# Depthwise convolution of a projection read straight from PSUM, block boundaries convolved together

## Chip, cores and metric

One NeuronCore of a Trainium2 chip runs the whole program. The metric is the device time of one execution in microseconds (us). The engines are named as in the profile: PE is TensorE (matrix products), PEld its weight loads, DVE is VectorE, ACT is ScalarE, POOL is GpSimd, SP is the queue that issues nearly all DMAs. Every engine works through its own instructions in a fixed order, and waits at one whose inputs or buffers aren't ready.

## What is computed

The reference is one layer of an encoder on 2048 tokens of width 1024: a normalised input goes through one projection, whose columns feed neighbourhood attention, an mLSTM and a gated delta rule; then come an output projection, cross-attention and a feed-forward layer. The change touches the delta rule's input alone: 1152 projected columns (q, k, v) go through a centred depthwise convolution over five tokens and a SiLU.

```python
def centred_depthwise_conv(x, w):
    c = x.shape[-1]
    return lax.conv_general_dilated(
        x, w[:, None, :].astype(x.dtype), window_strides=(1,),
        padding=[(CONV_K // 2, CONV_K // 2)],
        dimension_numbers=('NWC', 'WIO', 'NWC'), feature_group_count=c)
...
    qkv = jax.nn.silu(centred_depthwise_conv(jnp.concatenate([q, k, v], axis=-1), conv_w))
    qc, kc, vc = jnp.split(qkv, 3, axis=-1)
```

Token t of the output needs tokens t-2 to t+2 of the projection, so an output next to the boundary of two blocks of tokens needs projections of both blocks.

## The kernel before

The kernel is written in a framework that takes the program in the order of its source, gives each engine a fixed list of instructions by a list scheduler (earlier source goes first where several are ready), and sets the semaphores. Channels lie on the 128 partitions, tokens along the free dimension, everything in fp32; products are split in a high and a low part and take three passes.

`pass_a` (L153) is the stage around the change. It goes over four blocks of 512 tokens (b = 0 to 3). For each block it runs nine channel tiles (ct = 0 to 8) of `gdn_in` (L282); after tile 2 it normalises the next block's input (`norm_in`, L239), after tile 6 it makes the gates (`gates`, L335). Then come the Gram matrices of the block's pairs of chunks (`gram`, L412), which read the convolved q, k, v back from DRAM (`gd_c`), with projections of the mLSTM and of the attention (`ml_in`, `rest`) between them. The inverses of a group (`inv`, L475: 30 steps of two small DVE instructions for each direction, L495 and L496) stand in the source ahead of the next block, so they run on DVE beside the next block's convolutions.

One tile of `gdn_in` before the change:

- `wtile` (L982 on): the weights are loaded by SP, cast to `whi` on ACT (L987); the rest `wlo` is made by a POOL subtraction (L989) of 128 x 1024 elements from SBUF.
- `gemm` (L1018): 24 matmuls of 128 x 512 (L108) into a PSUM tile of the pool `psg`, which has two buffers, one bank each. The gates, the mLSTM and the attention projections use the same two.
- L295: ACT copies the bank to the SBUF tile `pad`, columns 4 to 515. The bank is free once that copy is done.
- L299 and L303: DVE copies the four tokens before the block in from `edge`, and this tile's last four tokens out to `edge` (27 each; memsets, L297 and L301, stand in at both ends of the sequence).
- L306 and L308: DVE multiplies by the first tap and adds the other four, five instructions with `pad` and `acc` in SBUF.
- L310: ACT makes the tanh; L311: DVE makes the SiLU (doubled) of it; L312: SP stores the tile to `gd_c`, two tokens behind the projection.

`pad`, `acc` and `th` have two buffers each (`cp`, L160).

## Time and profile before

| what | value |
|---|---|
| time, median of 3 runs | 3787.74 us (3775.37 to 3800.31) |
| span of the profiled execution | 3789.0 us |
| PE busy over the span | 3468.7 us (92%) |
| DVE busy over the span | 1819.1 us (48%) |
| ACT busy over the span | 1153.2 us (30%) |
| POOL busy over the span | 1601.0 us (42%) |

Busy shares are means over a program whose stages have different limits, so the stage of the change, the first 620 us, is to be read by itself. A busy PE is not a PE at its peak: matmuls overlap, and the clock that it is granted changes with what it did before. "Idle before" names what an engine waited for; it costs something only where that engine, or one that waits for it, sets the end.

### The profile page before, as it was taken

How to read it: one execution, taken by the hardware profiler on the slowest of the kernel's cores; microseconds unless marked ns; L12 is line 12 of the kernel's file. 1: busy time of each engine (PE TensorE's matmuls, PEld its weight loads, DVE VectorE, ACT ScalarE, POOL GpSimd, SP SyncE). 2: the span in 40 equal slices, each digit the busy share in tenths (PEclk: the TensorE clock that was granted, in tenths of full speed). 3: DMA queues.
4: the chain of work that ended last, by engine and by line, in shares of the span. 5: the costliest groups of instructions: out<-in, count | busy, mean ns of one | idle time of the engine just before them, and what ended most of it. 6: DMA issues, size and time to landing. Idle time of an engine off the chain costs nothing.

```text
span 3789.0 us, 54073 instructions
## 1 busy us (share of the span) xinstructions
PE 3468.7 (92%) x21392; PEld 2774.0 (73%) x21392; DVE 1819.1 (48%) x3257; ACT 1153.2 (30%) x2015; POOL 1601.0 (42%) x947
## 2 busy tenths in 40 slices
PE   5878688888788889999999999999999999999998
PEld 4656566666666655588888887888888778888887
DVE  7697977625666644553443436222222352222224
ACT  3233232232323333544343344222222332222223
POOL 4455444554454531253535445333333453333333
PEclk9988888988899996999999999999999999999999
DMA  4546475678999565742233233111111141111112
GB/s 140 179 132 183 140 193 142 174 181 200 202 215 217 173 216 172 210 174 98 95 134 134 87 123 133 53 45 48 45 50 48 60 138 48 49 53 48 53 47 89
DMA packets 396663, 466.07 MB, mean 123 GB/s; under 512 B 151978, under 2 KB 296826, under 8 KB 393338
## 3 DMA queue, kind: packets, MB, share of 16 engines
q1 hardware_dynamic: 392794, 450.55, 41.2%
q0 software_dynamic: 3616, 12.06, 0.9%
q8 instruction: 169, 2.77, 0.3%
q14 instruction: 84, 0.69, 0.1%
HBM read 360.01 MB, written 102.50 MB: 122 GB/s over the span
## 4 chain that ended last, share of the span: by engine, by line
PE 52%; DVE 1%; ACT 1%; issue 1%; DMA 0%; POOL 0%; POOLq 0%; DVEq 0%; SPq 0%; ACTq 0%
PE psg L108 31%; PE psa L108 21%; PE psa L1180 0%; DVE nh L1005 0%; DVE ss L1016 0%; PE psm L88 0%; PE psm L99 0%; ACT whi L987 0%; DMA out_y<-nh 0%; DMA xb<-x_d 0%; POOL wlo L989 0%; DVE xb L1251 0%; ACT acta L1137 0%; ACT acta L1006 0%; ACT sqt L1015 0%
## 5 line engine op out<-in xcount | busy, mean ns | idle before, releaser
L989 POOL TENSOR_TENSOR wlo<-wraw,whi 128x1024 fp32r<-128x1024 f32 (+2 forms) x401 | 842.0, 2101 | 1294.1 <-ACT whi L987 1271.7
L108 PE MATMUL psg<-acta,whi 128*128 128x512 f32 x3008 | 975.3, 404 | 36.9 <-ACT pad L295 23.2
L108 PE MATMUL psg<-actb,whi 128*128 128x512 f32 (+2 forms) x2752 | 857.4, 393 | 36.8 <-DVE rt L613 10.2
L987 ACT CAST whi<-wraw 128x1024 fp32r<-128x1024 f32 (+2 forms) x417 | 373.5, 896 | 1192.3 <-PE psa L108 551.7
L108 PEld LDWEIGHTS psg<-acta,whi 128*128 128x128 f32 x3008 | 576.7, 194 | 169.2 <-ACT pad L295 25.2
L108 PE MATMUL psa<-ht,whi 128*128 128x512 f32 x2048 | 638.6, 395 | 0.6 <-ACT whi L987 0.5
L108 PEld LDWEIGHTS psg<-actb,whi 128*128 128x128 f32 (+1 forms) x2752 | 518.9, 193 | 148.2 <-ACT pad L295 11.2
L108 PE MATMUL psg<-acta,wlo 128*128 128x512 f32 x1504 | 602.5, 402 | 3.6 <-POOL wlo L989 3.6
L108 PE MATMUL psg<-actb,wlo 128*128 128x512 f32 (+2 forms) x1376 | 539.9, 393 | 27.9 <-POOL wlo L989 27.9
L108 PEld LDWEIGHTS psa<-ht,whi 128*128 128x128 f32 x2048 | 384.0, 188 | 95.1 <-ACT whi L987 1.5
L1229 DVE TENSOR_TENSOR fr<-fr 128x512 f32<-128x512 f32 x128 | 167.9, 1312 | 495.4 <-ACT fr L1228 495.4
L1242 DVE TENSOR_TENSOR xb<-psa,xb 128x512 f32<-128x512 f32 x256 | 175.6, 691 | 476.4 <-PE psa L108 476.3
L108 PE MATMUL psa<-ht,wlo 128*128 128x512 f32 x1024 | 401.0, 396 | 0.7 <-POOL wlo L989 0.7
L108 PEld LDWEIGHTS psg<-acta,wlo 128*128 128x128 f32 x1504 | 290.8, 193 | 67.6 <-POOL wlo L989 5.0
L108 PEld LDWEIGHTS psg<-actb,wlo 128*128 128x128 f32 (+1 forms) x1376 | 265.2, 193 | 86.5 <-POOL wlo L989 33.4
L1232 POOL TENSOR_TENSOR ht<-fr,ht 128x512 fp32r<-128x512 f32 x128 | 169.1, 1321 | 249.1 <-ACT ht L1231 247.8
L108 PEld LDWEIGHTS psa<-ht,wlo 128*128 128x128 f32 x1024 | 192.3, 188 | 47.5 <-POOL wlo L989 1.8
L1016 DVE TENSOR_TENSOR ss<-ss,sqt 128x512 f32<-128x512 f32 (+1 forms) x91 | 123.4, 1356 | 47.0 <-ACT sqt L1015 44.3
L308 DVE SCALAR_TENSOR_TENSOR acc<-pad,vecs,acc 128x512 f32<-128x512 f32 (+2 forms) x144 | 143.6, 1000 | 1.5 <-DVE sm L436 0.6
L1231 ACT CAST ht<-fr 128x512 fp32r<-128x512 f32 x128 | 79.4, 621 | 180.1 <-DVE fr L1229 180.0
L1228 ACT ACTIVATE fr<-psg 128x512 f32<-128x512 f32 x128 | 75.9, 593 | 132.3 <-PE psg L108 132.3
L495 DVE TENSOR_TENSOR tv<-x 72x30 f32<-72x30 f32 (+36 forms) x210 | 94.4, 470 | 2.0 <-DVE x L496 0.6
(376 smaller groups left out, 3982.3 us busy)
## 6 DMA issues: line engine op xcount, KB each, us to landing
wraw<-in_w_ff SPq DMA_DIRECT2D x72, 512.0 KB
wraw<-in_w_ff SPq DMA_DIRECT2D x144, 256.0 KB
wraw<-in_w_gd SPq DMA_DIRECT2D x36, 512.0 KB
sc_d<-sc SPq DMA_DIRECT2D x32, 576.0 KB
xt<-in_xT SPq DMA_DIRECT2D x16, 1024.0 KB
wraw<-in_w_out SPq DMA_DIRECT2D x32, 512.0 KB
wraw<-in_w_xq SPq DMA_DIRECT2D x32, 512.0 KB
wraw<-in_w_xo SPq DMA_DIRECT2D x32, 512.0 KB
```

The costliest lines, as they stand in the source:

```text
L108: nc.tensor.matmul(out=out, lhsT=a(k), rhs=b(k), start=(i == 0), stop=(i == n - 1))
L308: V.scalar_tensor_tensor(out=acc[:, :n], in0=pad[:, p0 + j:p0 + j + n], scalar=cw(j), in1=acc[:, :n], op0=ALU.mult, op1=ALU.add)
L495: V.tensor_tensor(out=tv, in0=m[:, j + 1:32, j:j + 1].broadcast_to([2 * N, n, j]), in1=m[:, j:j + 1, 0:j].broadcast_to([2 * N, n, j]), op= ...
L987: nc.scalar.copy(out=hi, in_=raw)
L989: (lo_eng or nc.gpsimd).tensor_tensor(out=lo, in0=raw, in1=hi.bitcast(F32), op=ALU.subtract)
L1016: nc.vector.tensor_tensor(out=ss, in0=ss, in1=sq, op=ALU.add)
L1228: S.activation(out=r, in_=ps, func=AF.Relu)
L1229: V.tensor_tensor(out=r, in0=r, in1=r, op=ALU.mult)
L1231: S.copy(out=ht[:, 0], in_=r)
L1232: G.tensor_tensor(out=ht[:, 1], in0=r, in1=ht[:, 0].bitcast(F32), op=ALU.subtract)
L1242: V.tensor_tensor(out=xs[nb][:, j], in0=ps, in1=xs[nb][:, j], op=ALU.add)
```

## The change

The copy of the projection to SBUF goes away. ACT makes the first tap's product straight from the PSUM bank (`activation` with a scale per partition) for 508 of the block's 512 tokens; DVE adds the other four taps with the bank as an input. The first and the last four tokens of each tile's projection are copied by ACT into one SBUF tile `edge` for all tiles and blocks. After the nine tiles of a block a new function `gdn_edge` convolves the four tokens around the block's left boundary for all nine tiles together, and stores them with one DMA; the last block does so for both of its ends. The DVE memsets of `edge` at both ends of the sequence are done once at the start. (The file's comments are removed too; that changes no instruction.)

```diff
-            self.edge = [None, None]
+            self.edge = self.gp.tile([P, 9, 40], F32, name="edge")
+            for i in (0, 4):
+                self.nc.vector.memset(self.edge[:, :, 9 * i:9 * i + 4], 0.0)
...
+                for i in (3, 4) if b == 3 else (b,):
+                    self.gdn_edge(i)
                 t0, t1 = GROUPS[b]
...
         ps = self.gemm(self.wtile(I["w_gd"][ct], KT, "w"), act)
-        pad = self.cp.tile([P, 518], F32, name="pad")
-        S.copy(out=pad[:, 4:516], in_=ps)
-        if b == 0:
-            V.memset(pad[:, 2:4], 0.0)
-        else:
-            V.tensor_copy(out=pad[:, 0:4], in_=self.edge[0][:, ct])
-        if b == 3:
-            V.memset(pad[:, 516:518], 0.0)
-        else:
-            V.tensor_copy(out=self.edge[1][:, ct], in_=pad[:, 512:516])
         cw = lambda j: self.vecs[:, 64 + 5 * ct + j:65 + 5 * ct + j]
-        acc = self.cp.tile([P, 514], F32, name="acc")
-        V.tensor_scalar(out=acc[:, :n], in0=pad[:, p0:p0 + n], scalar1=cw(0), scalar2=None, op0=ALU.mult)
+
+        n = 508
+        acc = self.cp.tile([P, 508], F32, name="acc")
+        S.activation(out=acc, in_=ps[:, :n], func=AF.Copy, scale=cw(0))
+        S.copy(out=self.edge[:, ct, 8 * b + 4:8 * b + 8], in_=ps[:, 0:4])
+        S.copy(out=self.edge[:, ct, 8 * b + 8:8 * b + 12], in_=ps[:, 508:512])
         for j in range(1, 5):
-            V.scalar_tensor_tensor(out=acc[:, :n], in0=pad[:, p0 + j:p0 + j + n], scalar=cw(j), in1=acc[:, :n], op0=ALU.mult, op1=ALU.add)
...
+            V.scalar_tensor_tensor(out=acc, in0=ps[:, j:j + n], scalar=cw(j), in1=acc, op0=ALU.mult, op1=ALU.add)
+        th = self.cp.tile([P, 508], F32, name="th")
+        S.activation(out=th, in_=acc, func=AF.Tanh, scale=0.5)
+        V.scalar_tensor_tensor(out=acc, in0=th, scalar=1.0, in1=acc, op0=ALU.add, op1=ALU.mult)
+        nc.sync.dma_start(out=self.gd_c[ct, :, 512 * b + 2:512 * b + 510], in_=acc)
+
+    def gdn_edge(self, i):
+
+        nc, V = self.nc, self.nc.vector
+        cw = self.vecs[:, 64:109].rearrange("p (c j) -> p c j", j=5)
+        a, b, c = (self.cp.tile([P, 9, 4], F32, name=n, bufs=1) for n in ("ea", "eb", "ec"))
+        for j in range(5):
+            o = b if j else a
+            V.tensor_tensor(out=o, in0=self.edge[:, :, 8 * i + j:8 * i + j + 4], in1=cw[:, :, j:j + 1].broadcast_to([P, 9, 4]), op=ALU.mult)
+            if j:
+                V.tensor_tensor(out=a, in0=a, in1=b, op=ALU.add)
+        nc.scalar.activation(out=c, in_=a, func=AF.Tanh, scale=0.5)
+        V.scalar_tensor_tensor(out=a, in0=c, scalar=1.0, in1=a, op0=ALU.add, op1=ALU.mult)
+        x0, x1 = (2, 4) if i == 0 else (0, 2) if i == 4 else (0, 4)
+        nc.sync.dma_start(out=self.gd_c[:, :, 512 * i - 2 + x0:512 * i - 2 + x1].rearrange("c p l -> p c l"), in_=a[:, :, x0:x1])
```

## Rows read from the trace of the kernel before

**Rows 1.** Page, part 2: DVE's busy tenths in 40 slices of 94.7 us.

```profile
DVE  7697977625666644553443436222222352222224
```

**Rows 2.** Windows, convolution stretches: length, busy us (count) of PE PEld DVE ACT POOL.

```profile
43.00:116.00 73.00, 56.33 (x231) 42.80 (x230) 67.87 (x97) 25.82 (x34) 33.03 (x14) 0.86 0.37 109
...
172.00:262.00 90.00, 69.84 (x280) 52.98 (x281) 87.94 (x148) 26.17 (x34) 59.81 (x18) 0.87 0.52 148
...
333.00:430.00 97.00, 73.17 (x548) 55.44 (x546) 93.01 (x173) 31.17 (x45) 49.10 (x22) 0.82 0.62 174
...
514.00:620.00 106.00, 94.14 (x760) 71.60 (x758) 100.51 (x209) 33.27 (x54) 44.24 (x15) 0.94 0.54 149
```

**Rows 3.** Windows, tile pad on DVE: its busy us, first and last of four stretches.

```profile
43.00:116.00 73.00, 44.85 (x51) 0.86 0.37 109
...
514.00:620.00 106.00, 46.29 (x61) 0.94 0.54 149
```

**Rows 4.** Lines from 0 to 620 us: busy us and mean ns, then idle before.

```profile
L308 DVE SCALAR_TENSOR_TENSOR acc<-pad,vecs,acc 128x512 f32<-128x512 f32 (+2 forms) x144 | 143.6, 1000 | 1.5 <-DVE sm L436 0.6
...
L306 DVE TENSOR_SCALAR acc<-pad,vecs 128x512 f32<-128x512 f32 (+2 forms) x36 | 19.9, 552 | 3.8 <-DMA gd_c<-acc 2.9 <-ACT pad L295 0.8
L299 DVE COPY pad<-edge 128x4 f32<-128x4 f32 x27 | 19.2, 710 | 0.1
L303 DVE COPY edge<-pad 128x4 f32<-128x4 f32 x27 | 18.5, 685 | 3.2 <-ACT pad L295 3.1
```

**Rows 5.** Tile acc and line L1005: duration ns min/median/max of one instruction.

```profile
L308 DVE SCALAR_TENSOR_TENSOR acc<-pad,vecs,acc x144: 732/744/4902, 46.4 to 610.6; 128x512 f32<-128x512 f32 x72, 128x510 f32<-128x510 f32 x36, 128x514 f32<-128x514 f32 x36
...
L1005 DVE SCALAR_TENSOR_TENSOR nh<-xb,vecs,psm x64: 732/740/749, 1674.6 to 3088.4; 128x512 f32<-128x512 f32 x64
```

**Rows 6.** Timeline, 64 to 76 us, of DVE, POOL and PE: start, duration us, instruction, idle before.

```profile
64.68 7.65 DVE L308 SCALAR_TENSOR_TENSOR acc<-pad,vecs,acc 128x510 f32<-128x510 f32 x2
...
64.22 4.82 POOL L272 TENSOR_TENSOR actb<-xt,actb 128x2048 fp32r<-128x2048 f32 x1 [7.30 <-ACT actb L271]
69.00 2.78 POOL L989 TENSOR_TENSOR wlo<-wraw,whi 128x1024 fp32r<-128x1024 f32 x1
...
75.85 0.79 PE L108 MATMUL psg<-acta,whi 128*128 128x512 f32 x1 [8.98 <-ACT pad L295]
```

**Rows 7.** Waits, 0 to 640 us (SP: to 620): us in total, times, longest.

```profile
ACT th L310 <- DVE acc L308: 139.4, 29, 10.1
...
PE psg L108 <- ACT pad L295: 33.0, 7, 9.0
PE psg L108 <- POOL wlo L989: 28.4, 7, 11.0
...
SPq L312 <- DVE acc L311: 69.7, 16, 8.9
```

**Rows 8.** Timeline of ACT: first and last of 36 copies to pad and tanhs.

```profile
43.39 0.57 ACT L295 COPY pad<-psg 128x512 f32<-128x512 f32 x1
...
52.87 0.63 ACT L310 ACTIVATE th<-acc 128x510 f32<-128x510 f32 x1 [1.79 <-DVE acc L308]
...
597.17 0.58 ACT L295 COPY pad<-psg 128x512 f32<-128x512 f32 x1
...
611.41 0.64 ACT L310 ACTIVATE th<-acc 128x514 f32<-128x514 f32 x1 [5.68 <-DVE acc L308]
```

**Rows 9.** Chain of waits: a projection's 24 matmuls at full clock (start, us).

```profile
1755.37 5.49 PE psg L108 x24
```

**Rows 10.** Lines, and a DMA (us to landing): nearest rows for added work.

```profile
L437 DVE TENSOR_TENSOR sm<-beta,sm x11: 154/170/1712, 152.6 to 528.7; 128x12 f32<-128x12 f32 x11
...
L546 ACT ACTIVATE rt<-psg 128x512 f32<-128x512 f32 x16 | 9.4, 589 | 10.1 <-PE psg L108 10.1
...
L398 ACT ACTIVATE egl<-psx x4: 223/230/237, 129.6 to 627.2; 128x96 f32<-128x96 f32 x4
...
w_d<-z POOLq DMA_DIRECT2D x4, 192.0 KB, 9.4
```

More of the change, by code (lines that the diff above doesn't have):

```diff
@@ L287, in gdn_in @@
         act = self.acts[b % 2]
-        if ct == 0:
-            self.edge = [self.edge[1], self.cp.tile([P, 9, 4], F32, name="edge")]
-        n = (510, 512, 512, 514)[b]
-        p0 = 2 if b == 0 else 0
-        t0 = 512 * b - 2 + p0
-        ps = self.gemm(self.wtile(I["w_gd"][ct], KT, "w"), act)
-        pad = self.cp.tile([P, 518], F32, name="pad")
-        S.copy(out=pad[:, 4:516], in_=ps)
-        if b == 0:
-            V.memset(pad[:, 2:4], 0.0)
-        else:
-            V.tensor_copy(out=pad[:, 0:4], in_=self.edge[0][:, ct])
@@ L309, in gdn_in @@
-        th = self.cp.tile([P, 514], F32, name="th")
-        S.activation(out=th[:, :n], in_=acc[:, :n], func=AF.Tanh, scale=0.5)
-        V.scalar_tensor_tensor(out=acc[:, :n], in0=th[:, :n], scalar=1.0, in1=acc[:, :n], op0=ALU.add, op1=ALU.mult)
-        nc.sync.dma_start(out=self.gd_c[ct, :, t0:t0 + n], in_=acc[:, :n])
+        ps = self.gemm(self.wtile(I["w_gd"][ct], KT, "w"), act)
+        cw = lambda j: self.vecs[:, 64 + 5 * ct + j:65 + 5 * ct + j]
+        n = 508
+        acc = self.cp.tile([P, 508], F32, name="acc")
```

## The prediction

> **What bounds the kernel now.** I read four views in this order. The page's slices first: over the whole span DVE is busy 48%, but in the first seven slices it stands at 7, 6, 9, 7, 9, 7, 7 tenths [rows 1]; that is the stretch in which the changed function runs. Then the windows. `gdn_in`'s copies come in four bursts, one for each block, and I cut the stretches there: in all four DVE is busy 93 to 98%, together 349.3 of 366 us, while PE is busy 293.5 us at a granted clock of 0.82 to 0.94 [rows 2]. So DVE sets the pace there, and PE waits for it and runs partly at the lower of its two clock levels. A projection takes 5.49 us at full clock [rows 9]; the four stretches hold 40 of them (36 of the convolution, 4 of the gates), one each 9.15 us.
>
> Then the lines and single durations: what is DVE busy with? The tap instruction L308 has a median of 744 ns, but a mean of 1000 and a maximum of 4902 [rows 4, 5]; copies of four elements take 0.7 us in the mean [rows 4]. The timeline shows why: at 64.68 two taps take 7.65 us, and end where two POOL subtractions (4.82 and 2.78 us, both from SBUF) end [rows 6]. A DVE instruction that reads two SBUF tensors, or copies within SBUF, stands still while POOL works on SBUF. Last the waits: ACT's tanh waits 139.4 us for the taps, and behind it in ACT's order stand the next casts of weights and the next copy to `pad`, which frees the PSUM bank; PE waited 8.98 us for that copy in the same example [rows 6], 33.0 us in all, and 28.4 us for `wlo`, which stands behind ACT's cast [rows 7].
>
> **Removed from DVE.** 36 first taps (19.9 us) and 54 edge copies (19.2 + 18.5 us): 57.6 us [rows 4]. Rows overlap by some 0.07 us (the end of one row against the start of the next), so 90 instructions fewer give 57.6 - 6.3 = 51.3 us. 18 memsets are left out.
>
> **Taps from PSUM.** 144 stay, with the bank in place of `pad`. The nearest row is L1005: the same instruction, same size, one SBUF tensor, one PSUM tensor and a scalar per partition. It takes 732 to 749 ns, with POOL's subtractions of weights running beside it [rows 5]; its spread shows no standing still. Bounds: 740 ns, or the present mean of 1000 if the freedom from POOL doesn't carry over. I take 740: 144 x (1.000 - 0.740) = 37.4 us. [...]
>
> **Added.** `gdn_edge` runs five times: 9 small products and sums and one SiLU step on DVE, 50 instructions. The nearest row has 128 x 12 elements: median 170, maximum 1712 ns, since both inputs are in SBUF [rows 10]. Bounds: 50 x (0.17 - 0.07) = 5 us and, at the 0.42 us that its mean would be with the waits for POOL, 21 us; I take 10, nearer to the median. On ACT the first tap replaces the copy to `pad`: 0.59 us by the scaled read L546 against 0.57 [rows 8, 10]; its scale per partition may add some; even 0.1 us is 3.6 us on an engine that is busy a third of these stretches [rows 2]. 72 edge copies at up to 0.23 us [rows 10] are 17 us on ACT, which I cost at nothing in the total: ACT waits 139.4 us for DVE in this stretch [rows 7]. If that cover went, they would cost these 17 us. They do stand between the bank's filling and DVE's second tap, 0.46 us for each tile.
>
> DVE's sum: -51.3 - 37.4 + 10 = -78.7 us. The tile `pad` shows how much lies in the four stretches: 168.9 us on DVE (44.85 in the first, 46.29 in the fourth) of 201.2 in all, 84% [rows 3, 4]. So 0.84 x 88.7 = 74.5 us leave them and about half of `gdn_edge`, 5 us, comes in: 349.3 - 74.5 + 5 = 280 us of DVE work.
>
> **What sets the stretches then.** With DVE as tightly packed as now (95%) they would take 293 us, a gain of 73. But PE's 293.5 us stand there too. If they shrink with no better clock and PE is packed as DVE is now, 293.5 / 0.954 = 308 us: a gain of 58. PE becomes as much of a bound as DVE.
>
> **The bank is held longer.** This is the wait that is added: a bank was free after ACT's copy; now only after DVE's last tap, and PE's second next projection waits for it. On PE everything in its order stands behind that: gates, Gram matrices, mLSTM projections. With DVE free the hold is 0.59 + 0.46 + 4 x 0.74 = 4.0 us; with as much other DVE work between the taps, 7.0. Two banks then allow one projection in (5.49 + 7.0) / 2 = 6.2 us, under the 9.15 of now. The bursts of the next block's normalisation and the gates will exceed that; I take 8 us off for them, 2 a block, a choice. Gain 58 - 8 = 50.
>
> **Stores.** 36 tile stores stay on SP, slightly shorter; five are added, of 1152 pieces of 16 bytes (8 at both ends). SP's queue already stands behind the tile stores 69.7 us [rows 7], and weight loads behind them; those waits shrink with DVE's. An edge store waits for the last tile's edge, ten small DVE steps and a tanh; `gram`'s first load of the block waits for it. Landing: nothing beyond what tile stores take, or the 9.4 us of the zero fill of `w_d`, 192 KB in 1536 pieces of 128 bytes [rows 10]. I take 0 on the path: mLSTM projections fill PE's order between Gram matrices. Without that cover it is 4 x 9.4 = 38 us.
>
> The span would go from 3789.0 to 3739; the median of the runs lies 1.3 us below that span, so I forecast **3738 us**.
>
> **Rivals.**
>
> 1. *Little changes: PE's own order decides.* The waits for `wlo` and the half-speed matmuls stay, and only the 33.0 us that PE waits for ACT's copy [rows 7] go, while the edge stores cost 4 x 5 = 20 us (about half of their bound): 3789 - 33 + 20 - 1 = 3775. For it: PE is busy 80% of the stretches already [rows 2]. Against it: DVE's late tanhs are behind the `wlo` waits too.
> 2. *Slower: the bank.* The time from ACT's copy to the tile's tanh is now 9.5 us for the first tile and 14.2 for the last; over all 36 it has a mean of 16.7 [rows 8], since taps stand behind the inverses' chain, the normalisation and the tile before. If a bank is held for as long, a projection takes (5.49 + 16.7) / 2 = 11.1 us, 40 of them 444 us instead of 366: 3788 + 78 = 3866. It decides from a hold of 2 x 9.15 - 5.49 = 12.8 us; over 1% slower from 14.7. Against it: 16.7 us at one tile in 9.15 means that 1.8 tiles are queued at DVE, a queue that its relief shortens and two banks can't hold. [...]
> 3. *The taps stay as slow.* If a PSUM tap still stood still behind POOL, DVE would lose only 51.3 - 10 = 41 us, 34 in the stretches; they stay bound by DVE: 366 - 34 / 0.954 = 330, 3752, less 8 us for the bank: about 3760. The row of L1005 speaks against it; it counts with "within 1%".
>
> **Chances.** Forecast (3690 to 3750): 0.52. Rival 1: 0.20; rival 3: 0.07 (both within 1%, that is 3750 to 3826; about what a measurement of this kernel can tell from no change). Rival 2: 0.21. The range leaves out 0.05 below 3690 (a gain of 98 needs DVE's full 73 and a better clock of PE beyond) and some 0.13 of rival 2 above 3830: 3690 to 3830. Faster by over 1%: 0.52; within: 0.27; slower: 0.21.
>
> **What would show it.** Right: L308's successor at 740 ns with a maximum near 750; DVE's idle share in the convolution stretches well above 5% and these nearer to 79 than to 91 us each; PE's waits for ACT's `pad` gone and few waits for `acc`. Wrong: waits of PE for DVE `acc` of several us a tile, a granted clock under 0.82 (rival 2); taps of 2 us and more (rival 3); ACT's squares of `gram` waiting for the edge's store (rival 1). The list scheduler writes a new order for all engines, which I can't see; a worse order in later stages would upset the sum without any of these.

## The result, and the profile after

The changed kernel takes 3837.86 us (median of 4 runs, 3834.2 to 3846.1); the kernel before took 3781.55 us beside it. The ratio is 1.0143, 95% interval 1.0116 to 1.0171: it is slower by 54 us where I forecast 50 us faster, and the time lies above my range. The profiled execution has a span of 3844.3 us, 55.3 more than before.

Parts 1 and 2 of the page after, the answer to [rows 1]:

```profile
PE 3495.1 (91%) x21392; PEld 2795.8 (73%) x21392; DVE 1749.4 (46%) x3201; ACT 1161.7 (30%) x2092; POOL 1550.5 (40%) x947
...
DVE  6694947453666645553434445322222352222224
```

DVE is busy 1749.4 us instead of 1819.1. So the work that was to be saved is saved: 69.7 us of the 78.7 that I had worked out. It is the time that didn't follow. The windows of the four convolution stretches (length, busy us and count of PE, PEld, DVE, ACT, POOL, granted clock, DMA), the answer to [rows 2]; each reaches from about a block's first tap to its last tanh, while [rows 2] were cut at the copies to `pad` (both kernels by one cut follow further down):

```profile
43.00:114.00 71.00, 58.47 (x248) 44.64 (x247) 56.74 (x91) 30.00 (x55) 34.38 (x15) 0.95 0.46 128
163.00:283.00 120.00, 70.10 (x268) 53.01 (x267) 109.61 (x224) 37.01 (x61) 41.04 (x17) 0.79 0.49 121
364.00:473.00 109.00, 65.77 (x252) 50.52 (x251) 99.39 (x202) 26.34 (x51) 36.00 (x14) 0.80 0.41 108
561.00:656.00 95.00, 64.65 (x246) 48.61 (x246) 83.27 (x186) 27.39 (x53) 25.94 (x11) 0.86 0.46 109
```

Only the first block did what was forecast: DVE's busy share fell to 80%, the clock granted to PE rose to 0.95, and the last tanh starts at 113.4 us instead of 128.8. In the others PE is busy for 58 to 68% of the stretch; it waits. The tile `acc` after (L300 the four taps on DVE, L296 the first tap on ACT; below, who waited for the tile: us, times), and PE's waits from 0 to 900 us, the answers to [rows 5] and [rows 7]:

```profile
L300 DVE SCALAR_TENSOR_TENSOR acc<-psg,vecs,acc x144: 641/739/755, 43.5 to 655.0; 128x508 f32<-128x508 f32 x144
L296 ACT ACTIVATE acc<-psg,vecs x36: 664/677/687, 42.7 to 649.1; 128x508 f32<-128x508 f32 x36
...
  PE psg L108: 108.2, 17
...
PE psg L108 <- DVE acc L300: 108.2, 17, 19.2
...
PE psg L455 <- DMA kq<-gd_c: 8.6, 3, 3.3
```

The taps have a maximum of 755 ns: none stands still behind POOL any more. But PE waits 108.2 us for them, in place of 33.0 for ACT's copy. How a bank comes to be held so long is seen in the timeline of the longest of these waits (DVE from 224 to 242 us, then POOL and PE):

```profile
224.24 0.74 DVE L300 SCALAR_TENSOR_TENSOR acc<-psg,vecs,acc 128x508 f32<-128x508 f32 x1
...
225.68 1.88 DVE L263 TENSOR_REDUCE ss<-sq 128x256 f32<-128x1024 f32 x1
227.47 0.73 DVE L300 SCALAR_TENSOR_TENSOR acc<-psg,vecs,acc 128x508 f32<-128x508 f32 x1
228.13 1.25 DVE L270 SCALAR_TENSOR_TENSOR xt<-xt,vecs,psm 128x256 f32<-128x256 f32 x3
...
232.46 0.73 DVE L300 SCALAR_TENSOR_TENSOR acc<-psg,vecs,acc 128x508 f32<-128x508 f32 x1
233.12 1.91 DVE L263 TENSOR_REDUCE ss<-sq 128x256 f32<-128x1024 f32 x1
234.96 4.48 DVE L502 TENSOR_TENSOR tv<-x 72x228 f32<-72x228 f32 x1
239.36 0.73 DVE L300 SCALAR_TENSOR_TENSOR acc<-psg,vecs,acc 128x508 f32<-128x508 f32 x1
...
240.34 0.73 DVE L300 SCALAR_TENSOR_TENSOR acc<-psg,vecs,acc 128x508 f32<-128x508 f32 x1
...
234.55 4.50 POOL L276 TENSOR_TENSOR acta<-xt,acta 128x2048 fp32r<-128x2048 f32 x1 [4.62 <-ACT acta L275]
...
241.22 1.19 PE L108 MATMUL psg<-actb,whi 128*128 128x512 f32 x2 [19.25 <-DVE acc L300]
```

Between taps of 0.74 us stand the next block's normalisation (L263, L270) and the last group's inverses (L502); one of the latter takes 4.48 us beside a POOL subtraction of 4.50, standing still as the taps used to [rows 6]. PE stands idle for 19.25 us. From the first tap's start on ACT to the last tap's end on DVE, all 36 tiles have a mean of 10.6 us: 6.6 in block 0, 12.9, 13.6 and 9.5 in blocks 1 to 3. No inverses run in block 0.

The second new wait is at the boundary step. Timeline from 286 to 301 us, behind block 1's last tile (L317 ends the step, L319 is its store, L313 the first product of the *next* boundary's step, L424 a load of `gram`, L430 its square):

```profile
286.32 0.19 DVE L317 SCALAR_TENSOR_TENSOR ea<-ec,ea 128x36 f32<-128x36 f32 x1
...
286.88 0.37 SPq L319 DMA_DIRECT2D gd_c<-ea  x1
...
294.83 0.20 DVE L313 TENSOR_TENSOR ea<-edge,vecs 128x36 f32<-128x36 f32 x1 [8.32 <-DMA gd_c<-ea]
294.95 0.20 DVE L399 COPY gcg<-psx 128x48 f32<-128x48 f32 x1
...
295.14 1.01 SPq L424 DMA_DIRECT2D kq<-gd_c  x2
...
299.57 0.84 ACT L430 ACTIVATE sq<-kq 128x768 f32<-128x768 f32 x1 [3.38 <-DMA kq<-gd_c]
```

The first product of a boundary's step needs only the last four tokens of the block before. So the list scheduler puts it a whole block early, right behind the step before it. It writes `ea`, which has one buffer (`bufs=1` in the diff) and is still being stored: DVE stands for 8.32 us until the store lands, and behind it in DVE's order stand the gates (L399 on), on which the Gram stage depends as well. The load of `gram` (L424) waits for the same landing, whatever the buffers, and goes at 295.14. In the last block, which has two steps, the two landings stand in a row: the first store goes at 657.98, the next step's first product at 665.14, its store at 668.34, the load at 673.47. Waits of DVE and SP, 0 to 760 us:

```profile
DVE ea L313 <- DMA gd_c<-ea: 27.6, 4, 8.3
...
SPq L424 <- DMA gd_c<-ea: 16.0, 3, 6.7
```

This happens behind every block: 27.6 us on DVE, and 16.0 us in which SP's queue stands at `gram`'s load. From the end of a block's last tanh to its first square of `gram` it was 9.0, 9.1, 11.8 and 9.4 us; now it is 14.6, 16.2, 24.1 and 21.6, 37 us more in all.

So there were three theories. **H**: the bank is held through the taps. **E**: the boundary step and its store stand in front of the Gram stage. **O**: the list scheduler draws up a new order for all engines, and that alone moves the time. A good marker for the first stage is the first matmul of the scan behind it (the line of `pss<-wp,kb`; the number after the durations is its first start), 837.1 us before and 899.6 after:

```profile
L653 PE MATMUL pss<-wp,kb x768: 218/218/366, 837.1 to 1240.6; 64*64 64x64 f32 x192
```

```profile
L660 PE MATMUL pss<-wp,kb x768: 218/218/366, 899.6 to 1304.4; 64*64 64x64 f32 x192
```

The loss is complete there (62.5 us); what follows takes 7 us less than before.

Where in the first stage does it stand? Here both kernels are cut alike: from ACT's first read of a block's first bank to the block's last tanh. First the last of the four stretches and the sum of all four, before and after (columns as in [rows 2]):

```profile
514.30:611.40 97.10, 87.39 (x731) 66.61 (x730) 91.85 (x187) 30.44 (x50) 40.27 (x14) 0.93 0.56 152
sum 407.00, PE 322.45 PEld 246.18 DVE 390.49 ACT 122.56 POOL 205.65; mean PE 80.61 PEld 61.55 DVE 97.62 ACT 30.64 POOL 51.41
```

```profile
561.50:655.70 94.20, 64.38 (x244) 48.42 (x244) 82.51 (x182) 26.62 (x52) 25.94 (x11) 0.86 0.46 109
sum 392.50, PE 257.31 PEld 195.35 DVE 346.54 ACT 118.33 POOL 136.60; mean PE 64.33 PEld 48.84 DVE 86.64 ACT 29.58 POOL 34.15
```

Then what lies between them, up to the scan, before and after:

```profile
sum 386.70, PE 329.36 PEld 266.81 DVE 220.36 ACT 112.62 POOL 187.00; mean PE 82.34 PEld 66.70 DVE 55.09 ACT 28.16 POOL 46.75
```

```profile
sum 464.40, PE 411.10 PEld 334.93 DVE 199.45 ACT 125.81 POOL 207.94; mean PE 102.77 PEld 83.73 DVE 49.86 ACT 31.45 POOL 51.98
```

The stretches didn't become longer (392.5 us against 407.0); what lies between them did, by 78 us. In the stretches PE ran 1936 matmuls before and runs 1006 now. Those that left are mostly not projections: 832 matmuls of Gram matrices, inverses and the like stood among the projections before, and 68 do now. So PE waits for the taps in the stretches with nothing else in its order, and does that work behind them. A longer hold and a new order of PE go together here.

### The profile page after: what moved, and what is told of

It reads as the page before. It is cut to its first block, busy times and chain, and to the rows that moved or that the text cites. A ratio compares the mean times of both kernels' runs of the same rounds, so it can differ in the third digit from the quotient of the medians.

```text
span 3844.3 us, 54193 instructions
## 1 busy us (share of the span) xinstructions
PE 3495.1 (91%) x21392; PEld 2795.8 (73%) x21392; DVE 1749.4 (46%) x3201; ACT 1161.7 (30%) x2092; POOL 1550.5 (40%) x947
## 4 chain that ended last, share of the span: by engine, by line
PE 68%; DVE 12%; DMA 12%; issue 3%; SPq 2%; ACT 2%; POOL 1%; DVEq 0%; POOLq 0%; ACTq 0%
PE psg L108 39%; PE psa L108 20%; DVE tv L502 2%; DVE acc L300 2%; DVE x L503 2%; DMA ge<-g_row 2%; PE psn L955 1%; PE psy L974 1%; DMA sc<-v_d 1%; DMA ob<-ho_d 1%; PE pst L964 1%; DMA me<-mx_row 1%; DMA x<-x_d 1%; PE psx L531 1%; DMA gr<-g_row 1%
## 5 line engine op out<-in xcount | busy, mean ns | idle before, releaser
L996 POOL TENSOR_TENSOR wlo<-wraw,whi 128x1024 fp32r<-128x1024 f32 (+2 forms) x401 | 804.7, 2008 | 1403.3 <-ACT whi L994 1360.7
L108 PE MATMUL psg<-actb,whi 128*128 128x512 f32 (+2 forms) x2752 | 866.8, 396 | 89.9 <-DVE acc L300 73.9
L502 DVE TENSOR_TENSOR tv<-x 96x30 f32<-96x30 f32 (+36 forms) x210 | 112.8, 559 | 25.5 <-DMA x<-x_d 19.3
L300 DVE SCALAR_TENSOR_TENSOR acc<-psg,vecs,acc 128x508 f32<-128x508 f32 x144 | 105.7, 736 | 10.3 <-ACT edge L298 9.7
```

Of the source, the lines that this page charges most:

```text
L108: nc.tensor.matmul(out=out, lhsT=a(k), rhs=b(k), start=(i == 0), stop=(i == n - 1))
L300: V.scalar_tensor_tensor(out=acc, in0=ps[:, j:j + n], scalar=cw(j), in1=acc, op0=ALU.mult, op1=ALU.add)
L502: V.tensor_tensor(out=tv, in0=m[:, j + 1:32, j:j + 1].broadcast_to([2 * N, n, j]), in1=m[:, j:j + 1, 0:j].broadcast_to([2 * N, n, j]), op= ...
L996: (lo_eng or nc.gpsimd).tensor_tensor(out=lo, in0=raw, in1=hi.bitcast(F32), op=ALU.subtract)
```

## The experiments

Medians are of device us; each ratio is to the kernel before on the same chip, with its 95% interval. "Scan" is the marker. "Place" is the number of projection matmuls ahead of the attention's first matmul in PE's order, in which the kernel before has 2784.

| run | us | ratio (interval) | scan us | place |
|---|---|---|---|---|
| after | 3837.9 | 1.0143 (1.0116 to 1.0171) | 899.6 | 2808 |
| e1_copy | 3857.4 | 1.0173 (1.0139 to 1.0208) | 904.5 | 2760 |
| e2_lasttap | 3884.5 | 1.0254 (1.0222 to 1.0286) | 901.3 | 2592 |
| e3_third_bank | 3858.1 | 1.0181 (1.0154 to 1.0209) | 875.3 | 2759 |
| e4_taps_first | 3841.1 | 1.0146 (1.0115 to 1.0177) | 900.4 | 2808 |
| e5_edges_alone | 3834.9 | 1.0135 (1.0108 to 1.0162) | 897.5 | 2784 |
| e6_no_edges | 3812.7 | 1.0075 (1.0051 to 1.0099) | 821.5 | 2592 |
| e7_third_bank_no_edges | 3789.3 | 1.0016 (1.0001 to 1.0030) | 822.3 | 2760 |
| e8_order_only | 3801.9 | 1.0049 (1.0032 to 1.0067) | 853.5 | 2784 |
| e9_edges_late | 3807.3 | 1.0059 (1.0032 to 1.0086) | 868.4 | 2784 |
| e10_edges_late_bank | 3848.5 | 1.0170 (1.0139 to 1.0202) | 868.9 | 2759 |
| e11_block0 | 3819.1 | 1.0080 (1.0044 to 1.0116) | 818.1 | 2592 |
| e12_before_third_bank | 3840.8 | 1.0159 (1.0118 to 1.0201) | 871.1 | 2759 |
| e13_copies_no_step | 3793.8 | 1.0028 (1.0012 to 1.0045) | 845.3 | 2784 |
| e14_before_fill2 | 3801.0 | 1.0045 (1.0019 to 1.0071) | 835.0 | 2784 |
| e15_block0_fill2 | 3794.9 | 1.0029 (1.0010 to 1.0048) | 822.8 | 2784 |
| e16_no_edges_fill2 | 3823.3 | 1.0099 (1.0064 to 1.0134) | 829.2 | 2760 |
| e17_hold_alone | 3833.9 | 1.0144 (1.0108 to 1.0180) | 893.9 | 2784 |
| e18_edges_late_one_copy | 3830.6 | 1.0136 (1.0098 to 1.0175) | 853.8 | 2765 |

### First look: the copy, the last tap, a third bank, the priority

**e1_copy**, the changed kernel with the bank freed by a copy:

```diff
+        pad = self.cp.tile([P, 512], F32, name="pad")
+        S.copy(out=pad, in_=ps)
+        ps = pad
         S.activation(out=acc, in_=ps[:, :n], func=AF.Copy, scale=cw(0))
```

> The changed kernel with one step put back: ACT copies the bank to an SBUF tile (512 columns), and first tap, other taps and edge copies read that tile. ACT's first tap, gdn_edge and its stores stay. Theory H (a psg bank is held until DVE's last tap, 11.2 us in the mean, and PE waits for it 108 us where it waited 33 for ACT's copy): the bank is free after 0.6 us again, PE's waits for taps go, and the time falls below the changed kernel's 3838 by 55 or more, to 3740-3785, although the taps stand behind POOL again (mean near 1000 ns). Theory E (the edges: gdn_edge's small steps and its finely cut stores ahead of gram): stays at 3825-3845. Theory O (the list scheduler's new order, no single edit): anywhere, with PE's waits spread over many releasers.

3857 us, above the ranges of H and of E: no gain although the bank is free at once, so H is not the whole (the taps read SBUF again here; from the kernel before, with its mean of 1000 ns against 739, I estimate that their gain is gone too). The last tanh starts at 613.8 us, within 3 us of the kernel before, but the scan at 904.5. This order has 2176 projection matmuls ahead of the scan instead of 2040, which by an estimate are some 31 us (136 at 5.49 us for 24); the rest, 36 us, may lie in the boundary step, which this run doesn't show.

**e2_lasttap**, the kernel before with only the last tap from PSUM:

```diff
-        for j in range(1, 5):
+        for j in range(1, 4):
             V.scalar_tensor_tensor(out=acc[:, :n], in0=pad[:, p0 + j:p0 + j + n], ...)
+        m = min(n, 512 - p0)
+        V.scalar_tensor_tensor(out=acc[:, :m], in0=ps[:, p0:p0 + m], scalar=cw(4), in1=acc[:, :m], ...)
```

> The kernel before with one input moved: the copy to pad stays, four of the five taps read pad, and the last tap alone reads the PSUM bank, so that the bank is held until it. No edge of the change is in it. Theory H: holds of about the 16.7 us that lay between copy and tanh, shortened as PE falls back; PE waits for the tap instead of the copy; slower than before by 40 to 100 us, 3820-3880. Theory E: as before or some us faster (36 taps freed from POOL's lock, 36 x 0.26 = 9 us on DVE), 3770-3785.

96 us slower: H is real. 64 of them are there at the start of the scan, and 32 come later, where the attention had moved in PE's order (2592 in place of 2784). That second part belongs to O, so this run alone doesn't size H.

**e3_third_bank**, the changed kernel with a third bank for the projections, taken from the small products of gates and inverses, which now share a bank with the norms' sums:

```diff
-            self.sxps = pool("psx", 1, space=PSUM)
+            self.sxps = self.mps
+            self.gps2 = pool("psgx", 1, space=PSUM)
...
+            if self.gps2 is not None:
+                self.gi += 1
+            ps = self.gps2.tile([P, 512], F32, name="psgx") if self.gps2 is not None and self.gi % 3 == 0 else self.gps.tile(...)
```

> The changed kernel with a third bank for the projections in pass A: the tile psx (gates, inverses) shares the one bank of psm, and every third gemm goes to the bank so freed. Theory H: with three banks a projection needs (5.5 + 11.2) / 3 = 5.6 us instead of 8.4, so PE's waits for taps fall from 108 us to under 40: 3750-3795, if sharing psm costs nothing. Theory E: 3830 or more.

PE's waits for taps fall to 60 us and the last tanh comes 49 us earlier than in the changed kernel, as H says. The scan starts 24 us earlier. Yet the time isn't better (14 us worse by the ratios, with overlapping intervals), so part of the loss now lies behind the scan. The sharing and another order are both in here; e12 below tries them on the kernel before.

**e4_taps_first**, `high_priority(offset=3000)` around first tap, edge copies and taps:

> The changed kernel with ACT's first tap, the edge copies and the four taps of DVE put far ahead in the list scheduler's priorities (ahead of the inverses, the normalisation and the gates that stand earlier in the source). Nothing is computed otherwise. Theory H: the hold is long because other DVE work goes between the taps; it falls from 11.2 us towards 4 to 7, PE's waits for taps from 108 us to under 50, the time to 3770-3800. Theory E: no change, 3830-3845.

PE's order is that of the changed kernel but for 66 of 21392 matmuls, the mean hold stays at 10.5 us, and so does the time: the priority moved nothing that counts. Whether taps that are really in one piece would help, it can't tell.

### The boundary step taken apart

**e5_edges_alone**: the changed kernel with a copy of the bank and all five taps from SBUF on DVE, so that of the change only the boundary work is left.

```diff
+        pad = self.cp.tile([P, 512], F32, name="pad")
+        S.copy(out=pad, in_=ps)
+        ps = pad
-        S.activation(out=acc, in_=ps[:, :n], func=AF.Copy, scale=cw(0))
+        V.tensor_scalar(out=acc, in0=ps[:, :n], scalar1=cw(0), scalar2=None, op0=ALU.mult)
```

> The changed kernel, but ScalarE first copies the bank to a buffer of 512 columns in SBUF and all five taps run on VectorE from that copy: the bank is free after one copy, as before, and of the change only the common boundary step, its finely cut store and the copies beside it are left. Three theories. H (the bank is held through the taps, 11.2 us instead of 2.9): nothing of it is left, so the time is that of the kernel before, 3775 to 3795 us, and the tensor engine waits for the taps nowhere. E (the boundary step stands between the last tanh of a block and its first Gram step: 15.3, 16.9, 24.7 and 22.2 us there instead of 9.6, 9.7, 12.5 and 10.1): all of it is left, 3785 + 37 = 3822 us, and the four distances are those of the changed kernel. O (the order in which the program puts the instructions of all engines, drawn up anew for each kernel, moves the time by itself): any time up to 3860, with a loss that lies behind the convolutions, in no wait that H or E names.

51 us slower, with no wait of PE for taps left. The distances from the last tanh to the square are 13.6, 16.0, 23.2 and 29.6 us, and DVE waits for the step's store as in the changed kernel:

```profile
DVE ea L316 <- DMA gd_c<-ea: 26.7, 4, 10.1
```

So the waits of E are there where no bank is held. That they are what the time is lost to isn't shown by this run, since 2176 matmuls stand ahead of the scan here too, as in e1; e6, e9 and e13 speak to that.

**e6_no_edges** (no copies, no step; the tokens at the boundaries are left out) and **e7_third_bank_no_edges** (the same with the third bank):

```diff
-                for i in (3, 4) if b == 3 else (b,):
-                    self.gdn_edge(i)
...
-        S.activation(out=acc, in_=ps[:, :n], func=AF.Copy, scale=cw(0))
-        S.copy(out=self.edge[:, ct, 8 * b + 4:8 * b + 8], in_=ps[:, 0:4])
-        S.copy(out=self.edge[:, ct, 8 * b + 8:8 * b + 12], in_=ps[:, 508:512])
+        S.activation(out=acc, in_=ps, func=AF.Copy, scale=cw(0))
...
-        nc.sync.dma_start(out=self.gd_c[ct, :, 512 * b + 2:512 * b + 510], in_=acc)
+        nc.sync.dma_start(out=self.gd_c[ct, :, 512 * b:512 * b + 512], in_=acc)
```

> The changed kernel without the boundary step, its two copies per tile and its store; each tile stores 512 columns instead, so the four tokens around each block boundary are wrong and the others stand two tokens off: this part of the computation is left out. Taps, bank hold and tile loop stay. H: the time stays at that of the changed kernel, 3825 to 3845 us, and the tensor engine still waits some 110 us for the taps. E: 37 us come back, 3800, and the four distances from the last tanh to the first Gram square fall to some 10 us. O: it moves by some tens of us in a direction that neither names.

> The changed kernel with both suspects taken away: a third bank for the projections (the small products of the gates and of the inverses share a bank with the norms' sums for it), and no boundary step (its tokens are left out and the others stand two off, as in the run without the boundary step alone). If H and E are the whole loss, the cheaper taps and the missing edge copies are left: 3787 less 30 to 50, so 3735 to 3760 us. H without E: as the third bank alone gave, 3858. O: still over 3800, though the convolutions end no later than before (some 600 us) and each Gram step starts some 10 us behind its last tanh.

Without the boundary work 25 us come back (3812.7), as E expected less a part, though PE waits 93.7 us for taps. The scan even starts 15.6 us earlier than in the kernel before, and then the time ends 28 us above it: a loss behind the first stage that neither H nor E names. With the third bank as well (e7) the time is that of the kernel before within 6 us, but not the 30 to 50 under it that H and E together would give; it lies in none of the three ranges.

**e9_edges_late** computes everything, with the step behind two Gram steps that need no boundary token, and two buffers for its tiles:

```diff
+                order = ((1, 2, 0), (5, 6, 3, 4), (9, 10, 7, 8), (14, 13, 15, 12, 11))[b]
+                for k, t in enumerate(order):
+                    if k == 2:
+                        for i in (3, 4) if b == 3 else (b,):
+                            self.gdn_edge(i)
+                    self.gram(t)
...
-        a, b, c = (self.cp.tile([P, 9, 4], F32, name=n, bufs=1) for n in ("ea", "eb", "ec"))
+        a, b, c = (self.cp.tile([P, 9, 4], F32, name=n, bufs=2) for n in ("ea", "eb", "ec"))
```

> The changed kernel with the boundary step behind the first two Gram steps of its group, which are now two pairs of chunks that touch no boundary (order 1,2,0; 5,6,3,4; 9,10,7,8; 14,13,15,12,11), and with two buffers for the step's small tiles, so that the second step of the last block does not wait on VectorE for the first one's store. Everything is computed; bank hold and taps stay. E: the distances from a block's last tanh to its first Gram square fall from 15.3, 16.9, 24.7, 22.2 us to some 10 each, and about the 25 us come back that leaving the step out brought: 3805 to 3820 us; VectorE waits nowhere for the boundary store. H alone: nothing, 3838. O: some 20 us either way on top, as the order alone moved the kernel before by 18.

3807.3 us: 31 come back by moving the step, without leaving anything out. The distances from last tanh to first square fall only in part, to 14.6, 14.5, 10.4 and 13.1 us, where I expected some 10 each. DVE has no wait for `gd_c<-ea` left, SP's falls from 16.0 to 3.7 us, and PE's waits for taps stay:

```profile
PE psg L108 <- DVE acc L302: 97.6, 16, 16.8
...
SPq L426 <- DMA gd_c<-ea: 3.7, 1, 3.7
```

Which of its two edits did more, the buffers or the order, was not tried.

**e18_edges_late_one_copy**: one ACT copy for both edges of a tile instead of two, and I_FILL 3 to keep the attention near its place.

```diff
+        S.copy(out=self.edge[:, ct, 8 * b + 4:8 * b + 12].rearrange("p (s l) -> p s l", s=2), in_=ps.rearrange("p (s l) -> p s l", l=4)[:, 0:128:127])
```

> The run with the late boundary step (3807), with one copy of both edges per tile instead of two, and three pieces of projection work instead of two between the last inverses (I_FILL 3), which keeps the attention behind the 2765th projection matmul. The candidate that computes everything. If the copies on the bank cost: 10 us less than the late step alone, 3790 to 3800. If not: 3800 to 3815. O: 20 us either way.

It missed both ranges, and the cause stays open: the scan starts 15 us earlier than in e9, yet the ratio is 0.8% higher. I_FILL alone was not measured.

### The order by itself

**e8_order_only**, the kernel before with one GpSimd memset per tile that nobody reads:

```diff
+        tiny = self.cp.tile([P, 4], F32, name="tiny")
+        nc.gpsimd.memset(tiny, 0.0)
         th = self.cp.tile([P, 514], F32, name="th")
```

> The kernel before with one GpSimd memset of 4 columns per convolution tile into a buffer that nobody reads: 36 instructions that no one waits for, together a few us on an engine that idles for more than half the span; but the program's order on the tensor engine comes out different from the convolutions on. H and E: the time of the kernel before within 10 us, 3775 to 3795. O: a time more than 1% off, 3825 or more (or 3750 or less), from the order alone.

18 us slower, under the 1% that O named but clear of zero. 36 instructions that no one waits for, all done by 31 us, gave PE another order from the convolutions on, and the scan starts 16.4 us later. So the order alone is worth some 18 us here, and no single difference of that size between two of these kernels shows its cause. It is one order of many: how much another could cost, one such run doesn't tell.

**e12_before_third_bank** and **e10_edges_late_bank**: the third bank in the kernel before, and in e9.

> The kernel before with a third bank for the projections, got by letting the small products of the gates and inverses share the norms' bank: the price of that sharing by itself, since the kernel before holds its banks for one copy only and waits 33 us for it. H: the third bank brings at most these 33 us and the sharing costs nothing: 3755 to 3790. If the sharing costs (in the third bank's run of the changed kernel the inverses ended 29 us later behind the Gram steps than in the kernel before): 3800 to 3830. O: 20 us either way on top.

> As the run with the late boundary step, with the third bank for the projections too. H and E: what the run without both showed with wrong tokens, 3789, so 3780 to 3800 us, now with everything computed; the tensor engine waits under 50 us for the taps. E alone: no better than the run with the late boundary step. O: 3810 or more, as in the third bank's run (3858), whose loss lay behind the Gram steps.

The kernel before becomes 53 us slower with the third bank (above the range for a sharing that costs); 34 of them are there at the scan. PE's waits in e12 name a part: the gates stand in the shared bank (`psm`) behind the normalisation, 12.4 us (L350).

```profile
PE psm L527 <- DMA m<-wt_d: 14.8, 4, 8.6
...
PE psm L350 <- DVE xt L269: 12.4, 1, 12.4
```

The other line, the last inverses' wait for a load, is hardly longer than in the kernel before:

```profile
PE psx L524 <- DMA m<-wt_d: 12.4, 5, 4.0
```

In e10 PE's waits for taps fall from e9's 97.6 to 54.3 us and the scan starts where e9's does, yet it ends 41 us later, so its loss lies behind the first stage. What in e12 is the sharing and what the new order isn't shown, and none of e3, e7 and e10 says what a free third bank would bring.

**e11_block0**: the kernel before, with PSUM taps in block 0 alone and no boundary step at all (the tap to the left of the bank's first column is left away by a shorter range):

```diff
+        if b == 0:
+            S.activation(out=acc[:, :n], in_=ps[:, 0:n], func=AF.Copy, scale=cw(2))
+            S.copy(out=self.edge[1][:, ct], in_=ps[:, 508:512])
+            for j, a in ((0, 2), (1, 1), (3, 0), (4, 0)):
+                V.scalar_tensor_tensor(out=acc[:, a:n], in0=ps[:, a + j - 2:n + j - 2], scalar=cw(j), in1=acc[:, a:n], ...)
```

> The kernel before, with the convolution read from PSUM in the first block alone, where no inverses run on VectorE: ScalarE makes the middle tap for 510 columns, VectorE adds the four others, those to the left on shorter ranges, so there is no boundary step at all; blocks 1 to 3 as before. H: in the first block of the changed kernel the bank was held 5 to 9 us and its last tanh came 15 us earlier (113.4 instead of 128.8); that gain stays, the later blocks lose nothing: 3787 - 15 = 3770 us, and the last tanh of the first block at some 114 us. E: the same, there is no boundary step. If the gain of 15 us is given back before the scan, since the tensor engine sets the pace of the later blocks: 3780 to 3790. O: 20 us either way on top.

The first stage did gain: last tanh of block 0 some 15 us earlier, start of the scan 19 us earlier. The time is 30 us worse by the ratio. PE's timeline shows one place where it went:

```profile
1270.72 1.20 PE L99 MATMUL psm<-ident,rs 128*128 128x128 f32 x4 [7.33 <-DVE xt L266]
1291.37 1.25 PE L954 MATMUL psn<-nak,naqb 64*128 64x264 f32 x4 [19.45 <-DMA naqb<-nac_d]
```

The attention's first matmul now stands ahead of the last twelve projection tiles in PE's order and waits 19.45 us there for its queries. In e6, with the same place, it is 10.5 us.

**e14, e15, e16**: twice the projection work between scan steps (`B_FILL = 2`), which puts the attention back, for the kernel before, e11 and e6.

> The kernel before with two pieces of projection work instead of one between two scan steps (B_FILL 2): the same work, the attention at the same place among the projections on the tensor engine as in the next two runs. It is the mark for them. H and E: 3787 within 15 us. O: it may lie 20 us off by itself.

> Block 0 alone from PSUM, with two pieces of projection work between scan steps: the attention now stands behind the 2784th projection matmul as in the kernel before, no longer behind the 2592nd. O: the 19 us gained at the start of the scan reach the end: 15 to 25 us under the kernel before with the same fill, so 3760 to 3775, and the wait for the first queries (19.5 us) is gone. If the loss lies elsewhere: 3800 to 3820 as before.

> The changed kernel without any boundary work (tokens at the boundaries left out, the others two off), with two pieces of projection work between scan steps: the attention stands behind the 2760th projection matmul instead of the 2592nd. O: the 15 us gained at the start of the scan reach the end, 10 to 20 us under the kernel before with the same fill, and the loss of the changed kernel is then the boundary work alone, in spite of the held bank. H as the main price: 3800 or more.

The fill by itself costs the kernel before 17 us (e14). e11's loss is mostly gone (30 us to 11, by the ratios) with the wait; but the 19 us gained did not come out as the gain that O named: e15 is 6 us under e14 with overlapping intervals, and not under the kernel before. e16 came out in the range that I had given H, no better than e6, though the wait for queries fell from 10.5 to 4.1 us. Its scan starts 5.8 us before that of e14 and it ends 20 us later, so the loss lies behind the scan, where no convolution holds a bank. Why the later stages take back what the first gains stays open.

### Sizing the bank with the later order kept

**e17_hold_alone**: the kernel before, where each bank is kept until the fourth tap by a sum of two columns that nobody reads.

```diff
             V.scalar_tensor_tensor(out=acc[:, :n], in0=pad[:, p0 + j:p0 + j + n], ...)
+            if j == 3:
+                tiny = self.cp.tile([P, 1], F32, name="tiny")
+                V.tensor_tensor(out=tiny, in0=ps[:, 0:1], in1=acc[:, 0:1], op=ALU.add)
```

> The kernel before, where after the fourth tap (j = 3) VectorE adds one column of the bank and one of the accumulator into a column that nobody reads: 36 instructions of some 0.07 us, 3 us together, that keep each bank until the fourth tap is made, with all taps as before from SBUF. Behind the first stage its order on the tensor engine is that of the kernel before. H: the held bank has its full price without the gain of the cheaper taps: the run with the copies and no boundary step came out 9 us above the kernel before with some 37 to 58 us gained on the taps, so here 40 to 70 us are lost: 3825 to 3855. If the held bank is nearly free and that gain was lost elsewhere: 3787 to 3800.

**e13_copies_no_step**: e6 with the two edge copies left in.

> The changed kernel with the two edge copies per tile, but without the common boundary step and its store; the tiles store 512 columns as in the run without the boundary step, so the tokens at the boundaries are left out and the others stand two off. From the end of the first stage on, its order on the tensor engine has the scan, the attention and the output heads at the same places among the projections as the kernel before. If the step and its store are the price of the boundary work: the scan starts where it did without copies, 820 to 830 us, and the end is 3787 less 10 to 15, so 3770 to 3780 us. If the two copies on the bank are: the scan starts at 850 or later, and the time is 3800 or more. O: with the same order behind the first stage, the end moves by as much as the start of the scan (837 us in the kernel before).

Both have the scan, the attention and the output heads at the same places among the projections as the kernel before, so they are to be read by the first stage alone. e17 came out in H's range, e13 between its two cases. e17's waits and scan:

```profile
PE psg L108 <- DVE tiny L311: 139.9, 25, 16.9
...
L656 PE MATMUL pss<-wp,kb x768: 218/218/366, 893.9 to 1292.7; 64*64 64x64 f32 x192
```

and e13's:

```profile
PE psg L108 <- DVE acc L298: 84.5, 14, 18.8
...
L658 PE MATMUL pss<-wp,kb x768: 218/218/365, 845.3 to 1238.2; 64*64 64x64 f32 x192
```

In the five kernels with that later order (before, e8, e9, e13, e17) the time follows the start of the scan: 16, 31, 8 and 57 us later there, 19, 22, 11 and 54 us more in the end (each ratio times 3784). That makes them comparable, and they give the account. e13 has the cheaper taps and the held bank (11.0 us in the mean) and no boundary step: +11. The changed kernel adds the step and its store: 44 more, together +54. From e13 to the changed kernel the last tanh of blocks 0 to 3 starts 0, 10, 28 and 40 us later and the scan 54, so the step's price grows block by block, as E says.

e17, where the taps read SBUF as in the kernel before (1000 ns in the mean there), holds each bank for 12.7 us in the mean and costs 54 us; PE waits 139.9 us for its banks. So a held bank costs time, but 54 isn't its price in the changed kernel: with the cheaper taps (739 ns) the hold is shorter, 10.6 us in the mean. Nor is it the hold apart from the order: in e17's stretches, cut as above, PE runs 1029 matmuls instead of 1936, so Gram matrices and inverses moved behind them as in the changed kernel. No run has the cheaper taps without a longer hold, so +11 can't be divided into a gain and a loss. The two steps of the account close by construction, each may have some 18 us or more of the order in it, and e13's tiles hold other tokens.

## Why the prediction was wrong

- **What bounds the kernel, and the taps: right.** The taps take 739 ns against a forecast of 740, with a maximum of 755, so the wait for POOL is gone and rival 3 falls. `pad`'s work left DVE, `gdn_edge`'s instructions have medians of 0.19 us, near the 0.17 of my lower bound, ACT's first tap 0.677 us against 0.59. For this instruction a PSUM source costs no time that the traces show: a median of 739 ns for 508 columns from PSUM, of 744 for 510 to 514 columns from SBUF.
- **DVE's relief as a gain of 58 us: right in kind, its size not shown.** DVE's work fell by 69.7 us, and block 0, with the shortest holds and no inverses, ends 15 us earlier. But the four stretches, cut alike, shrank by 14.5 us and not by 58.
- **The bank, 8 us: the first step that failed.** Relief and bank together were to give -50; without the boundary step they give +11 (e13), 61 us off. I took the hold as the sum of its own instructions, 4.0 to 7.0 us. That holds in block 0 (6.6); elsewhere it is 9.5 to 13.6, since taps are single entries in DVE's order and inverses, norms and reductions stand between them. A row that says so was in my hands: copy to tanh took 16.7 us in the mean. I argued that the queue would shrink with DVE's load; the queue is an order fixed beforehand, and with 70 us less on DVE the same time is 11.2 us. Then I compared a mean hold with a break-even of 12.8 us. PE waited 108 us at a mean below that: 11 of the 36 holds are above it, and a short one doesn't give back what a long one cost. e17, which holds each bank until the fourth tap (12.7 us in the mean), is 54 us slower, with what its order costs in it.
- **The boundary step, 0 us: the second.** It measures 25 (left out with its copies, e6), 31 (moved, e9) and 44 (left out, e13), near the 38 that I had put as its bound without cover. I took the mLSTM projections on PE as its cover. They were none: the distances from last tanh to first square grew by 37 us: the step's own chain, then the landing for which `gram`'s load waits (16.0 us on SP). I also left out a wait that the diff shows: `ea` has one buffer, is read by a DMA, and is written again by the next step, 27.6 us of DVE with the gates behind. In the last block it puts two landings in a row; how much it costs in the others, where the load waits for the same landing, wasn't tried.
- **Rivals.** Rival 2 (the bank) is the right mechanism, though the hold stayed under the 12.8 us from which it was to decide. In rival 1 I had the edge stores at 20 us, on the path, but let the bank go free. The two together were not among the cases, and they make the whole of the difference: +11 + 44 = +55 instead of -50 + 0.
- **The order.** My last sentence let a worse order upset the sum. It is shown to move this kernel (e8, e11). Behind the scan the changed kernel loses nothing, but within the first stage PE's order is another one, with the Gram matrices and inverses behind the stretches; how much of each term is the order's stays open.

None of the versions that compute everything is faster than the kernel before. Of those with taps from PSUM, e15 (block 0 alone, 1.0029) and e9 (all blocks, 1.0059) come nearest.

## What to carry to other kernels

When several instructions read a PSUM bank in place of one copy, the bank's hold is not their sum (4.0 us by my estimate) but their spread in that engine's order (10.6 us in the mean here, 11 of 36 above 12.8): read it from the trace of before as the time from the first to the last of them, tile by tile, and compare the long ones, not the mean, with what the banks allow. The load of what a small store had just written waited for its landing here (16.0 us of SP's queue), and a small tile with one buffer made the next writer wait for it too: the scheduler had hoisted that writer, and its whole engine stood there (27.6 us of DVE). Two buffers, and the step behind work that doesn't need it, brought 31 us here together. And before a difference of half a per cent is explained, see what an edit that does nothing costs: here 18 us.

## What was not expected of the hardware

The boundary store's 1152 pieces of 16 bytes took 7 to 8 us from issue to landing (issued at 286.88, DVE released at 294.83; 481.57 and 489.62; 657.98 and 665.14), not much less than the 9.4 us of 192 KB in pieces of 128 bytes, issued by POOL [rows 10], though it is 18 KB.
